# Holding stationary operands over consecutive matmuls, and loading four tiles ahead of the first store, in a running logsumexp

## The chip, the cores and the metric

One core of a Trainium2 chip. The metric is the time on the device in microseconds (us); medians of several runs are given, and of each kernel one execution was profiled. Ratios are the mean time of one kernel's fast runs over that of the other's of the same rounds, so they are not quite the ratio of the medians quoted beside them. The span of a profile is some 2 us shorter than the timed run.

## The reference, cut to what matters

```python
x: float32 [4, 4096, 4128]          # batch, sequence, columns
out[:, 0, :] = x[:, 0, :]
for t in range(1, 4096):
    mx = maximum(out[:, t-1, :], x[:, t, :])
    out[:, t, :] = mx + log(exp(out[:, t-1, :] - mx) + exp(x[:, t, :] - mx))
```

It is a running log of a running sum of exponentials along the sequence. 270.5 MB are read and as many are written.

## The kernel before

A tile ("step") is 128 partitions of three rows each (two in one step of each batch), 4128 columns wide: 6.34 MB in, and as many out, in the same buffer. ScalarE writes the exponentials as float16 over the tile, TensorE makes the running sums with triangular stationary operands (`incl`, `excl`, `ident`) and carries the last row over from the step before (`pick`), ScalarE takes the log back into the tile. There are four buffers.

```python
def mm(pt, w, rhs, start=False, stop=False):
    nc.tensor.matmul(pt, lhsT=w, rhs=rhs, start=start, stop=stop, skip_group_check=True)
...
for i in range(r):                       # small products of the last 32 columns
    e = self.e(i, CH, CH + tail)
    mm(qt[:, i:, :], incl, to(e, r - i), start=i == 0)
    if i:
        mm(qt[:, :i, :], excl, to(e, i))
...
ahead = bufs - 1                         # bufs = 4
for s in steps[:ahead]:
    s.load()
...
if k.c == last and d + 1 == k.t.r:       # the last piece of a step is done
    k.t.store()
    if stored + ahead < len(steps):
        steps[stored + ahead].load()
    stored += 1
```

All loads and stores are issued by SyncE, one after the other, into one queue that sixteen DMA engines serve.

The softmax here doesn't subtract the row's maximum and nothing guards it: scores larger than these inputs give would overflow.

## Time and profile before

| | before |
|---|---|
| time, median of the first 3 runs | 1262.91 us (1262.84 to 1263.04) |
| span of the profile | 1261.0 us |
| DMA queue, share of 16 engines | 99.4%, 541.07 MB |
| ScalarE / TensorE / weight loads / VectorE busy | 75 / 55 / 19 / 36% |

The views are read in the order: who is full (shares), what the compute engines wait for, in which order the queue is served, and what single stretches look like. The prediction shows those lines. The first is a row of the page's DMA queues (packets, MB, share), of a queue that carries no data of the kernel:

```profile
q8 instruction: 18, 0.29, 0.1%
```

A row of ScalarE's timeline: its first work on the last tile (start, duration, ..., and in brackets the idle time before and what ended it). It tells when the last load had landed:

```profile
1220.78 1.91 ACT L128 ACTIVATE xt<-xt 128x2048 f16<-128x2048 f32 x1 [1.34 <-DMA xt<-in_x_dram]
```

### The profile page before, as it was taken

What the parts mean: (1) busy time and instruction counts of PE and PEld (TensorE: products, weight loads), DVE (VectorE), ACT (ScalarE), POOL (GpSimd) and SP (SyncE); (2) the same over time, 40 slices, a digit from 0 to 9 for tenths busy, and PEclk for the clock granted to TensorE, in tenths of its full rate; (3) what the DMA queues carried; (4) which work ended last, traced back from release to release, by engine and by line L of the source; (5) the groups of instructions that cost most, each with busy time, mean ns of one, the idle gap of its engine ahead of it and who ended that gap; (6) DMA issues with size and microseconds to landing.
All of it is one profiled execution on the core that took longest, in us unless ns stands there. A gap on an engine that the chain in (4) does not pass through costs nothing.

```text
span 1261.0 us, 6165 instructions
## 1 busy us (share of the span) xinstructions
PE 688.7 (55%) x2268; PEld 237.0 (19%) x2268; DVE 451.4 (36%) x445; ACT 947.3 (75%) x733; POOL 2.2 (0%) x13
## 2 busy tenths in 40 slices
PE   3665554555555555655346555555634755664552
PEld 1222111111121111211112211111211211221120
DVE  2443333333333333334424333333442433333344
ACT  5997777777777777778569777777966977777794
POOL 0000000000000000000000000000000000000000
PEclk9887777777677777777768777787777777778786
DMA  9999999999999999999999999999999999999998
GB/s 411 410 439 431 432 427 434 438 430 432 433 437 431 432 432 436 432 427 436 431 433 436 437 429 431 436 436 432 430 434 435 432 431 432 434 435 431 433 422 347
DMA packets 12702, 541.46 MB, mean 429 GB/s; under 512 B 1408, under 2 KB 1408, under 8 KB 1408
## 3 DMA queue, kind: packets, MB, share of 16 engines
q1 hardware_dynamic: 12672, 541.07, 99.4%
q8 instruction: 18, 0.29, 0.1%
q14 instruction: 12, 0.10, 0.0%
HBM read 270.53 MB, written 270.53 MB: 429 GB/s over the span
## 4 chain that ended last, share of the span: by engine, by line
DMA 69%; ACT 21%; PE 5%; issue 2%; DVE 1%; SPq 0%; ACTq 0%
DMA xt<-in_x_dram 67%; ACT xt L128 11%; ACT xt L162 10%; PE pt L88 5%; DMA out_dram<-xt 2%; ACT xt L167 0%; SPq L116 0%; DVE carry L92 0%; DVE carry L93 0%; ACTq L231 0%; SPq L113 0%; ACTq L128 0%; PE qt L88 0%
## 5 line engine op out<-in xcount | busy, mean ns | idle before, releaser
L128 ACT ACTIVATE xt<-xt 128x3072 f16<-128x3072 f32 (+3 forms) x176 | 478.5, 2719 | 247.9 <-DMA xt<-in_x_dram 247.8
L88 PE MATMUL pt<-xt,ident 128*128 128x512 f16 x672 | 251.3, 470 | 530.7 <-ACT xt L162 530.4
L162 ACT ACTIVATE xt<-pt 128x1024 f32<-128x1024 f32 x512 | 487.6, 1030 | 2.5 <-PE pt L88 0.7
L92 DVE CAST carry<-pt 32x1024 f16<-32x1024 f32 x176 | 216.4, 1230 | 761.0 <-ACT xt L162 760.7
L88 PE MATMUL pt<-xt,excl 128*128 128x512 f16 x672 | 247.0, 504 | 0.0
L93 DVE TENSOR_TENSOR carry<-pt,carry 32x1024 f16<-32x1024 f32 x176 | 215.9, 1227 | 6.1
L88 PEld LDWEIGHTS <-ident 128*128 128x128 f16 x672 | 70.1, 104 | 677.7 <-issue 654.0
L88 PE MATMUL pt<-xt,incl 128*128 128x512 f16 x352 | 152.0, 526 | 23.6 <-ACT xt L128 15.0
L88 PEld LDWEIGHTS <-excl 128*128 128x128 f16 x756 | 92.5, 124 | 141.0 <-issue 108.1
L88 PE MATMUL pt<-carry,pick 128*128 128x512 f16 x320 | 109.8, 429 | 0.0
L88 PEld LDWEIGHTS <-incl 128*128 128x128 f16 x480 | 45.2, 111 | 129.7 <-DVE carry L93 95.2
L88 PEld LDWEIGHTS <-pick 128*128 128x128 f16 x360 | 40.6, 113 | 57.0 <-issue 34.3
L167 ACT ACTIVATE xt<-qt 128x96 f32<-128x96 f32 (+1 forms) x44 | 10.9, 249 | 45.7 <-PE pt L88 45.7
L92 DVE CAST carry_t<-qt 32x32 f16<-32x32 f32 x44 | 8.7, 197 | 25.5 <-ACT xt L167 25.4
L88 PE MATMUL qt<-xt,incl 128*128 128x64 f16 (+2 forms) x128 | 12.3, 196 | 0.0
L88 PE MATMUL qt<-xt,excl 128*128 128x64 f16 (+1 forms) x84 | 10.6, 187 | 0.0
L93 DVE TENSOR_TENSOR carry_t<-qt,carry_t 32x32 f16<-32x32 f32 x44 | 8.5, 193 | 1.5
L88 PE MATMUL qt<-carry_t,pick 128*128 128x96 f16 (+1 forms) x40 | 8.2, 204 | 0.0
L83 DVE MEMSET carry<- 128x512 uint32 x4 | 1.9, 485 | 1.1 <-PEq L220 1.0
L70 ACT ACT_TABLE_LOAD x1 | 1.3, 1283 | 0.8 <-PEq L220 0.8
L35 POOL TENSOR_SCALAR_AFFINE_SELECT pick<-pick 128x128 f16<-128x128 f16 x2 | 0.6, 294 | 0.1
L25 POOL TENSOR_SCALAR_AFFINE_SELECT incl<-incl 128x128 f16<-128x128 f16 x1 | 0.3, 294 | 0.0
(11 smaller groups left out, 1.9 us busy)
## 6 DMA issues: line engine op xcount, KB each, us to landing
xt<-in_x_dram SPq DMA_DIRECT2D x40, 6192.0 KB, 42.2
out_dram<-xt SPq DMA_DIRECT2D x40, 6192.0 KB, 28.1
xt<-in_x_dram SPq DMA_DIRECT2D x4, 4128.0 KB, 37.3
out_dram<-xt SPq DMA_DIRECT2D x4, 4128.0 KB, 23.0
```

Source lines behind the costliest of these rows:

```text
L25: nc.gpsimd.affine_select(out=t, in_=t, pattern=[[1, P]], compare_op=mybir.AluOpType.is_ge, fill=0.0, base=base, channel_multiplier=-1,)
L35: nc.gpsimd.affine_select(out=t, in_=t, pattern=[[step, P]], compare_op=mybir.AluOpType.not_equal, fill=1.0, base=base, channel_multiplier=1,)
L70: nc.scalar.preload_act_table_set("natural_log_exp_and_others")
L83: nc.vector.memset(t, 0.0)
L88: nc.tensor.matmul(pt, lhsT=w, rhs=rhs, start=start, stop=stop, skip_group_check=True)
L92: nc.vector.tensor_copy(cr[HI:HI + 32, :], pt[HI:HI + 32])
L93: nc.vector.tensor_tensor(out=cr[LO:LO + 32, :], in0=pt[HI:HI + 32], in1=cr[HI:HI + 32, :], op=mybir.AluOpType.subtract,)
L128: nc.scalar.activation(self.t.half[:, :, 2 * c0:2 * c0 + w], self.t.xt[:, :, c0:c0 + w], ACT.Exp,)
L162: nc.scalar.activation(t.xt[:, j, c * CH:(c + 1) * CH], pt, ACT.Ln)
L167: nc.scalar.activation(t.xt[:, :, t0:D], self.qt, ACT.Ln)
```

## The change

Its intent: a matmul that uses the same stationary operand as the one before it needs no weight load, and with four loads ahead of the first store each store is due one load later.

```diff
+    held = [None]
+
     def mm(pt, w, rhs, start=False, stop=False):
-        nc.tensor.matmul(pt, lhsT=w, rhs=rhs, start=start, stop=stop, skip_group_check=True)
+
+        if held[0] is not w:
+            nc.tensor.matmul(pt, lhsT=w, rhs=rhs, start=start, stop=stop, skip_group_check=True)
+            held[0] = w
+            return
+        pe = nc.tensor
+        pe.add_instruction(mybir.InstMatmult(
+            name=nc.get_next_instruction_name(),
+            ins=[pe.lower_ap(rhs), pe.lower_ap(w, for_matmul_weights=True)],
+            outs=[pe.lower_ap(pt, opt=True)],
+            start_tensor_calc=start, stop_tensor_calc=stop, ldweights=False,
+            tile_size=(P, P), tile_position=(0, 0), bass_skip_group_check=True,
+        ))
 ... (cut)
             for i in range(r):
-                e = self.e(i, CH, CH + tail)
-                mm(qt[:, i:, :], incl, to(e, r - i), start=i == 0)
-                if i:
-                    mm(qt[:, :i, :], excl, to(e, i))
+                mm(qt[:, i:, :], incl, to(self.e(i, CH, CH + tail), r - i), start=i == 0)
+            for i in range(1, r):
+                mm(qt[:, :i, :], excl, to(self.e(i, CH, CH + tail), i))
 ... (cut)
-    for s in steps[:ahead]:
+    for s in steps[:bufs]:
         s.load()
 ... (cut)
-                    if stored + ahead < len(steps):
+                    if bufs <= stored + ahead < len(steps):
                         steps[stored + ahead].load()
```

## The prediction

> **What bounds the kernel now.** I read the page's shares first, then its DMA rows, then the list of waits, then the DMA queue's own order of time, and last some stretches. In the shares no compute engine is full, while the sixteen DMA engines are, in all slices but the last; the one data queue holds 99.4% of the span:
>
> ```profile
> PE 688.7 (55%) x2268; PEld 237.0 (19%) x2268; DVE 451.4 (36%) x445; ACT 947.3 (75%) x733; POOL 2.2 (0%) x13
> ...
> DMA  9999999999999999999999999999999999999998
> ...
> q1 hardware_dynamic: 12672, 541.07, 99.4%
> ```
>
> The reader is to see two things: DMA is the bound, and there is one weight load for each matmul (2268 and 2268). The waits say on what the compute engines stand. ScalarE stood 247.8 us for loads, and 0.7 us for the main matmuls:
>
> ```profile
> ACT xt L128 <- DMA xt<-in_x_dram: 247.8, 42, 12.2
> ...
> ACT xt L167 <- PE pt L88: 45.7, 44, 1.1
> ...
> ACT xt L162 <- PE pt L88: 0.7, 1, 0.7
> ```
>
> So TensorE holds up ScalarE by 46.4 us at most, ScalarE waits five times as long for data, and the data comes at the rate of the queue. Third, the start of the DMA queue's order of time (start, duration of issuing, line):
>
> ```profile
> 0.80 1.33 SPq L113 DMA_DIRECT2D xt<-in_x_dram  x3
> 37.00 0.35 SPq L116 DMA_DIRECT2D out_dram<-xt  x1
> 37.39 0.44 SPq L113 DMA_DIRECT2D xt<-in_x_dram  x1
> 63.44 0.34 SPq L116 DMA_DIRECT2D out_dram<-xt  x1
> 63.88 0.38 SPq L113 DMA_DIRECT2D xt<-in_x_dram  x1
> 86.17 0.34 SPq L116 DMA_DIRECT2D out_dram<-xt  x1
> ```
>
> Call the loads L0, L1, ... and the stores S0, S1, ...; the order is L0 L1 L2, S0 L3, S1 L4, S2 L5, and so on. From there a pair comes every 29.25 us or so, and the page has 42.2 us from a load's issue to its landing and 28.1 us for a store. A load issued at time t lands at t + 42.2, and the next pair is issued at t + 29.25: at each new pair some 13 us of work still lie in the queue. It does not run dry. Fourth, three stretches (busy time of PE, PEld, DVE, ACT, POOL; granted clock, DMA share, GB/s): the end's gap, the last stores, and the long middle:
>
> ```profile
> 1226.00:1234.00 8.00, 5.18 (x17) 1.84 (x17) 3.32 (x6) 7.89 (x8) 0.00 (x0) 0.79 0.44 188
> 1234.00:1261.00 27.00, 4.99 (x24) 1.78 (x22) 12.31 (x12) 8.41 (x9) 0.00 (x0) 0.69 0.91 391
> 300.00:1200.00 900.00, 495.57 (x1626) 170.40 (x1626) 316.82 (x312) 675.84 (x522) 0.00 (x0) 0.76 1.00 433
> ```
>
> The middle runs at 433 GB/s with share 1.00. The whole time adds up from it. Bytes: 541.07 MB / 433 GB/s = 1249.6 us. Gap at the end, where the last but one store waits for its compute: 8 x (1 - 188/433) = 4.5 us. The last stores below the rate: 27 x (1 - 391/433) = 2.6 us. The first 100 us, at 419 GB/s by the same view: 100 x (1 - 419/433) = 3.2 us, start included. Sum 1259.9; the span is 1261.0, the timed median 1262.91 (1.9 us outside the span).
>
> **What the Trainium skill says.** "Perfetto Trace Analysis", Roofline, bounds a core that is alone by its 16 DMA engines, about 435 GB/s together; the trace agrees with 433 in the middle. "DMA: Bandwidth & Descriptors", Queues, rings and completion order, says that each DMA engine consumes the descriptors of a ring in order. The trace fits: three loads issued together at 0.80 come one after the other (ScalarE's first work on L0 starts at 13.08, on L1 at 27.68), so an order of issue is an order of service. "TensorE: Matmul & The Clock Gate", LDWEIGHTS, gives columns / 1.2 in ns, so 107 for 128 columns; the group of ident has 104. The same page, Architectural detail, says that PE pulls weight loads ahead of matmuls in flight. The trace shows them hidden: in
>
> ```profile
> 49.32 1.03 PE L88 MATMUL pt<-xt,excl 128*128 128x512 f16 x4
> 50.19 0.59 PE L88 MATMUL pt<-carry,pick 128*128 128x512 f16 x2
> ```
>
> four matmuls with a load each take (50.19 - 49.32) / 4 = 217 ns apiece at a clock of 1.00, which is 512 columns at 2.35 columns per ns and leaves no room for 104 ns of loading.
>
> **Part one, weights held.** By the diff a matmul with the same weights as the one before asks for no load. But the order in which the built program's instructions stand says otherwise. In the changed program, 816 matmuls are made by the old call and 1452 by the new branch, and all 2268 still have a weight load directly before them: 260 of incl, 536 of excl, 496 of ident and 160 of pick come from the new branch. Whatever builds the program puts a load before each matmul, flag or not. I therefore expect 2268 loads in the trace and 237 us of PEld as before. Were the loads gone, 260 x 111 + 536 x 124 + 496 x 104 + 160 x 113 ns (the means of the four groups) = 165 us of PEld would go, all of it beside matmuls. On the path: 0 us either way. What is real is that in the tail's small products all three incl ones now come before the three excl ones: 84 products of some 190 ns change places within groups of five or so, at the same count: 0 us.
>
> **Part two, L3 ahead of S0.** The listing of the queue has one row moved: L0 L1 L2 L3, S0, S1, L4, S2, L5. From S1 on the order is the same as before, with the same four buffers. So "each store one load later" holds for the first store alone; S1 comes after L0 to L3 in both. Step by step, from rows above: L1 landed at 27.68, a full tile takes 6.34 MB / 433 = 14.6 us and the small first one 9.8 us, so L2 lands at about 42.3. Before: S0 until 52, L3 until 66.7. After: L3 until 57, S0 until 66.7: the same bytes, swapped. S0 is still issued at 37.0 and S1 at 63.4, since ScalarE works without a pause from 27.68 to 93.6 in the trace, on data that has landed: it does not wait for L3. L4 needs S0 landed, as it takes its buffer; S0 lands some 3 us after S1 is issued, so L4 is issued at about 67 and no longer at 63.88. That is a new wait of 3 us, but S1's 14.6 us lie in the queue meanwhile: nothing runs dry, 0 us. S2 at 86.2 and L5 at 86.6 come as before, and the rest with them, the gap of 4.5 us at the end too.
>
> One small cost: the first 42 us hold loads alone. Their rows say 406 GB/s for 0 to 28 us and 396 for 28 to 42, so 16.9 MB in some 40 us after the start, 421 GB/s against 433. Loads alone for one more tile would cost 14.6 x (433/421 - 1) = 0.4 us. A second: at 63.4 only 3 us of S0 remain, and the DMA engines do not all end together (in the gap at the end their share falls over some 6 us, from 1226 to 1232); a few may idle a little. I put 0.1 us on that. In sum 0 + 0 + 0.4 + 0.1, less rounding and chance: 1263.2 us.
>
> **Rivals.** First, that the weight loads do go on the chip, and TensorE's path shortens. For it: the chain of waits has 5% of PE, 63 us. Against it: the chain goes back from L-loads whose issue waits for a store's compute, while the queue has 13 us in hand; the chain follows releases, not the bound. And the listing has all loads. It would make of the time 1262 to 1263, since at 100% DMA a faster TensorE only waits longer; at the end, where TensorE holds ScalarE by about 0.7 us a few times, perhaps 1 us less. Second, that the deeper start carries through and keeps the queue fuller, so that the gap at the end closes: 4.5 us less, 1258.4. Against it: the order from S1 on is the same, and the gap comes from the last tiles' compute after the last landing at 1220.8, not from the start. Third, that the new wait of L4 for S0 does dry the queue: S0 would have to land over 14 us after S1's issue. If it did, by as much as 5 us, 1268. Fourth, fewer loads alter the granted clock (0.76 in the middle): 0 us, as TensorE is not on the path.
>
> **Range and chances.** Runs of one kernel lie within 0.2 us here. The uncertainty is in how the DMA engines drift apart after the swap and how the gap at the end falls: about 2.5 us each way. So 1260.5 to 1266.0. For 2%, 25 us, DMA would have to lose or save 11 MB worth of time; no rival reaches it. Faster 0.01, within 0.98, slower 0.01.
>
> **What would show it right or wrong.** Right: 2268 weight loads and about 237 us of PEld; 433 GB/s in the middle; four loads issued at once at 0.8; S0 near 37, S1 near 63.4, L4 near 67, waiting for S0's store; S2 near 86; a gap of about 4.5 us near 1230. Step one is wrong if PEld shows 816 loads or some 72 us; step two if S1 or S2 moves by over 3 us, or if the DMA share falls below 0.9 anywhere before 1200. The prediction is wrong if the rate of the middle itself changes with the new order, which I have nothing against but the equal order of the queue.

## The result

The changed kernel takes 1262.76 us (1262.53 to 1262.87, 6 runs), the kernel before 1262.95 us (1262.84 to 1263.08, 6 runs). The ratio is 0.9998, with a 95% interval of 0.9985 to 1.0011: the same. The page of the changed kernel has the same shares, and as many weight loads:

```profile
PE 690.7 (55%) x2268; PEld 236.3 (19%) x2268; DVE 451.4 (36%) x445; ACT 947.0 (75%) x733; POOL 2.2 (0%) x13
...
q1 hardware_dynamic: 12672, 541.07, 99.4%
q8 instruction: 18, 0.29, 0.1%
```

PEld is 236.3 us in 2268 loads where it was 237.0 us in 2268: no operand is held on the chip. Its waits (engine and line, what it waited for, us in all, times, longest) answer to those of before one by one, under new line numbers:

```profile
ACT xt L142 <- DMA xt<-in_x_dram: 247.8, 42, 11.8
...
ACT xt L180 <- PE pt L96: 46.3, 44, 1.1
...
ACT xt L175 <- PE pt L96: 0.7, 1, 0.7
```

The start of its DMA queue, in order of time:

```profile
0.80 1.91 SPq L127 DMA_DIRECT2D xt<-in_x_dram  x4
37.23 26.77 SPq L130 DMA_DIRECT2D out_dram<-xt  x2
69.00 0.34 SPq L127 DMA_DIRECT2D xt<-in_x_dram  x1
86.40 0.33 SPq L130 DMA_DIRECT2D out_dram<-xt  x1
```

Four loads go out at once, S0 at 37.2 and S1 at 63.7 (the second of the row of two, which ends at 64.0 and takes 0.3 us). L4 goes out at 69.0 and no longer at 63.88. S2, at 86.4 for 86.17, is back in the old order. Last, the same three stretches as before, and the landing of the last tile:

```profile
300.00:1200.00 900.00, 493.75 (x1624) 168.74 (x1623) 316.83 (x311) 675.67 (x522) 0.00 (x0) 0.77 1.00 433
1226.00:1234.00 8.00, 5.96 (x17) 1.96 (x16) 2.92 (x5) 7.53 (x8) 0.00 (x0) 0.71 0.44 188
1234.00:1261.00 27.00, 5.40 (x24) 1.90 (x22) 12.67 (x12) 8.79 (x9) 0.00 (x0) 0.69 0.91 391
```

```profile
1220.72 1.91 ACT L142 ACTIVATE xt<-xt 128x2048 f16<-128x2048 f32 x1 [1.34 <-DMA xt<-in_x_dram]
```

The middle has 433 GB/s as before, the gap at the end 188 as before, and the last tile lands 0.06 us from where it landed.

### The profile page after: what moved, and what is told of

Same layout as the page of the kernel before. It is cut to its first block, busy times and chain, and to the rows that moved or that the text cites. A ratio compares the mean times of both kernels' runs of the same rounds, so it can differ in the third digit from the quotient of the medians.

```text
span 1261.0 us, 6165 instructions
## 1 busy us (share of the span) xinstructions
PE 690.7 (55%) x2268; PEld 236.3 (19%) x2268; DVE 451.4 (36%) x445; ACT 947.0 (75%) x733; POOL 2.2 (0%) x13
## 4 chain that ended last, share of the span: by engine, by line
DMA 72%; ACT 19%; PE 5%; issue 2%; DVE 1%; SPq 0%; ACTq 0%
DMA xt<-in_x_dram 67%; ACT xt L142 10%; ACT xt L175 9%; DMA out_dram<-xt 5%; PE pt L96 3%; PE pt L92 2%; DVE carry L106 0%; DVE carry L107 0%; ACT xt L180 0%; SPq L130 0%; ACTq L244 0%; SPq L127 0%; ACTq L142 0%; PE qt L92 0%
## 5 line engine op out<-in xcount | busy, mean ns | idle before, releaser
L142 ACT ACTIVATE xt<-xt 128x3072 f16<-128x3072 f32 (+3 forms) x176 | 478.2, 2717 | 247.9 <-DMA xt<-in_x_dram 247.8
L92 PE MATMUL pt<-xt,ident 128*128 128x512 f16 x176 | 76.6, 435 | 493.7 <-ACT xt L175 493.7
L96 PE MATMUL pt<-xt,ident 128*128 128x512 f16 x496 | 203.7, 477 | 35.4 <-ACT xt L175 34.7
L96 PE MATMUL pt<-xt,excl 128*128 128x512 f16 x496 | 187.6, 496 | 0.0
L92 PE MATMUL pt<-xt,incl 128*128 128x512 f16 x176 | 92.2, 524 | 23.5 <-ACT xt L142 15.1
L92 PE MATMUL pt<-xt,excl 128*128 128x512 f16 x176 | 93.4, 531 | 0.0
L96 PE MATMUL pt<-xt,incl 128*128 128x512 f16 x176 | 92.9, 528 | 0.0
L92 PE MATMUL pt<-carry,pick 128*128 128x512 f16 x160 | 72.0, 450 | 0.0
L96 PE MATMUL pt<-carry,pick 128*128 128x512 f16 x160 | 68.5, 428 | 0.0
L180 ACT ACTIVATE xt<-qt 128x96 f32<-128x96 f32 (+1 forms) x44 | 10.9, 248 | 46.3 <-PE pt L96 46.3
L92 PEld LDWEIGHTS <-incl 128*128 128x128 f16 x220 | 22.6, 103 | 118.0 <-DVE carry L107 95.3
L92 PEld LDWEIGHTS <-excl 128*128 128x128 f16 x220 | 26.8, 122 | 36.8 <-issue 27.9
L96 PEld LDWEIGHTS <-incl 128*128 128x128 f16 x260 | 27.8, 115 | 10.9 <-issue 4.8
```

Of the source, the lines that this page charges most:

```text
L96: pe.add_instruction(mybir.InstMatmult(name=nc.get_next_instruction_name(), ins=[pe.lower_ap(rhs), pe.lower_ap(w, for_matmul_weights=True) ...
L142: nc.scalar.activation(self.t.half[:, :, 2 * c0:2 * c0 + w], self.t.xt[:, :, c0:c0 + w], ACT.Exp,)
L180: nc.scalar.activation(t.xt[:, :, t0:D], self.qt, ACT.Ln)
```

## The experiments

The theory that I took in: the bytes at the rate of the DMA queue set the time, neither part of the change touches that, and the one place where compute holds up the queue is a gap of 4.5 us at the end. The rivals: TensorE's weight loads are on the path after all; two effects of the change cancel; the queue's lead matters. There were twelve runs, each with the kernel before on the same chip (1262.94 to 1262.98 us there).

### E1: the operands truly held

The load that the build puts before every matmul is taken out again where it repeats the one before, after the program is scheduled. The result is correct.

```diff
+    for f in nc.m.functions:
+        for b in f.blocks:
+            kept, last_w = [], None
+            for i in b.instructions:
+                if type(i).__name__ == "InstLdweights":
+                    w = str(i.ins[0])
+                    if w == last_w:
+                        continue
+                    last_w = w
+                kept.append(i)
+            if len(kept) < len(b.instructions):
+                b.instructions = kept
     r = _run(nc, [arrays], core_ids=[0])
```

> The changed kernel, with the 1452 repeated weight loads taken out of the built program, so that the intent of the change is met: 816 loads for 2268 matmuls. My theory (DMA sets the time, loads are hidden beside matmuls): PEld falls from about 236 us to 70 to 75 us, the time stays within 0.5 us of 1262.8, the middle stays at 433 GB/s, and ScalarE still waits about 248 us for loads of data. Rival (TensorE's part of the chain of waits is real time): 1262.8 less up to 20 us. A third outcome: at the end, where ScalarE waits for TensorE, up to 1 us is saved.

Measured: 1261.47 us (1261.41 to 1261.66, 5 runs), ratio 0.9988 (0.9976 to 1.0001). The times of the two kernels lie apart by 1.5 us with spreads of some 0.5 us, though the interval still touches 1. From its page, and its first work on the last tile:

```profile
PE 688.7 (55%) x2268; PEld 86.8 (7%) x816; DVE 451.4 (36%) x445; ACT 947.1 (75%) x733; POOL 2.2 (0%) x13
...
q8 instruction: 12, 0.20, 0.1%
```

```profile
1219.53 1.91 ACT L142 ACTIVATE xt<-xt 128x2048 f16<-128x2048 f32 x1 [1.17 <-DMA xt<-in_x_dram]
```

150 us of weight loads are gone, a little less than the 165 expected: that sum took the means of the four groups, and over all loads of before these come to 248.4 us where 237.0 were busy. The time falls by a hundredth of that, but by more than the 0.5 us that my theory allowed. It did not come through TensorE: ScalarE's waits for TensorE are as before (46.3 us for the small products, where before had 45.7). It came in the data: the last tile landed 1.25 us earlier. And the row of the instruction queue has 12 packets for 18.

### E2: every weight load twice

```diff
     def mm(pt, w, rhs, start=False, stop=False):
+        nc.tensor.ldweights(w)
         nc.tensor.matmul(pt, lhsT=w, rhs=rhs, ...)
```

> The kernel before, with one more weight load ahead of every matmul: 4536 loads. My theory: PEld doubles to about 470 us and the time stays within 1 us of 1262.9, as two loads of 104 ns still fit beside a matmul of 217 ns and as TensorE is not on the bound. Rival (weight loads are on the path): the time rises by a good part of 2268 x 104 ns = 236 us, at least 20 us.

Measured: 1267.30 us (1266.94 to 1267.92, 4 runs), ratio 1.0033 (1.0018 to 1.0049). Both expectations miss: 4.3 us is more than the 1 us of my theory and a small part of 236. PEld was busy for 341.5 us in 4536 loads, where 470 was expected. From its page and its timeline:

```profile
q8 instruction: 27, 0.44, 0.1%
```

```profile
1224.91 1.91 ACT L129 ACTIVATE xt<-xt 128x2048 f16<-128x2048 f32 x1 [1.44 <-DMA xt<-in_x_dram]
```

Again ScalarE's wait for the small products did not grow (45.5 us), and the last tile landed later, by 4.13 us. This pointed to another theory, F: TensorE's instructions are themselves fetched by the 16 DMA engines, in packets of 16 KB, and a kernel that fills these engines pays for them. "Runtime: NRT & Kernel Launch", Instruction fetch mechanics, has the refill in 16 KiB blocks of 256 instructions, by a DMA queue of the sequencer's own. The numbers agree: the trace of before has 4586 instructions of TensorE, so 17.9 blocks, and the page has 18 packets; E1's 3134 make 12.2, with 12 packets; E2's 6853 make 26.8, with 27.

### E3: the early load alone

The two lines of the diff on loads, on the kernel before; weights and order of matmuls untouched.

> The kernel before with only the fourth load put ahead of the first store; weights and order of matmuls untouched. My theory: the same as the changed kernel, 1262.8 within 0.4 us, with L4 issued near 69 us after a wait for S0 of some 5 us. Rival (two parts of the change of opposite sign cancel): the time differs from 1262.8 by 2 us or more.

Measured: 1262.84 us (1262.54 to 1263.10, 4 runs), ratio 0.9999 (0.9985 to 1.0013). As my theory had it: nothing cancels.

### E4: the last two tiles' stores cut by columns

```diff
+        def store_part(self, c):
+            a, z = c * CH, D if c == last else (c + 1) * CH
+            nc.sync.dma_start(out=self.dram(out)[:, :, a:z], in_=self.xt[:, :, a:z])
 ...
-                if k.c == last and d + 1 == k.t.r:
+                if k.t in steps[-2:]:
+                    if d + 1 == k.t.r:
+                        k.t.store_part(k.c)
+                elif k.c == last and d + 1 == k.t.r:
                     k.t.store()
```

> The kernel before, with the stores of the last two tiles cut into four by columns, each issued as soon as its columns are done. My theory (the gap of 4.5 us near 1230 is the only place where compute holds up the queue): the gap closes and the time falls by 3 to 4.5 us, to 1258.4 to 1260. Rival (the gap is the engines' uneven ends, or smaller pieces of 4 KB a row cost more than they save): 1262 or longer.

Measured: 1271.54 us (1270.99 to 1272.14, 5 runs), ratio 1.0069: slower by 8.6 us. The experiment failed in its making. ScalarE's timeline has a new wait, for a store of its own tile:

```profile
1253.50 1.96 ACT L132 ACTIVATE xt<-xt 128x2112 f16<-128x2112 f32 x1 [18.06 <-DMA out_dram<-xt]
```

The exponential of the last columns waited 18 us for the store of other columns. Three strided pieces of one tile interleave in address, and the pieces are taken to overlap by the program that places the waits (argued from the wait, not tested by itself). It says nothing about the gap; E11 repeats it with pieces that don't interleave.

### E5: a copy, without compute

```diff
-    stored = 0
-    chunks[0].exp()
-    ... (all of the pipeline)
+    for i, s in enumerate(steps):
+        s.store()
+        if i + ahead < len(steps):
+            steps[i + ahead].load()
```

> The kernel before with all compute left out: the same loads and stores in the same order through the same four buffers. The result is wrong on purpose (the output is a copy of the input). My theory (the bytes at the queue's rate set the time): only the gap at the end and a little drift go, so 1256 to 1260 us at 433 GB/s in the middle. Rival (compute in the pipeline holds the queue back all along): 1240 us or less.

Measured: 1258.83 us (1258.33 to 1259.63, 4 runs), ratio 0.9966 (0.9951 to 0.9981). Its output is wrong, which doesn't matter for the time. All compute together, with the fetch of its instructions, costs 4.1 us of 1263. So no change to TensorE has more than about that to gain while the bytes move like this. Its queues (packets, MB, share) have almost no fetch of instructions:

```profile
q1 hardware_dynamic: 12672, 541.07, 99.7%
q14 instruction: 1, 0.01, 0.0%
```

### E6: three buffers

```diff
-    bufs = 4
+    bufs = 3
```

> The kernel before with three buffers, so two loads ahead. My theory (a store is issued 15.9 us after the next tile's landing, and with four buffers some 13 us of queued work cover that): with three nothing covers it, the queue runs dry in every step, and a step takes 15.9 + 14.6 + 14.6 + about 2 = 47 us where it took 29.25, in all 1900 to 2050 us, with a DMA share of about 0.65 in the middle. Rival (the queue keeps itself full whatever the lead): within 5% of 1263 us.

Measured: 2018.63 us in one look. Its queue in order of time, two pairs, and a stretch in the middle:

```profile
318.96 0.34 SPq L116 DMA_DIRECT2D out_dram<-xt  x1
319.40 0.38 SPq L113 DMA_DIRECT2D xt<-in_x_dram  x1
366.48 0.34 SPq L116 DMA_DIRECT2D out_dram<-xt  x1
366.91 0.38 SPq L113 DMA_DIRECT2D xt<-in_x_dram  x1
```

```profile
900.00:1100.00 200.00, 62.47 (x205) 21.66 (x205) 41.85 (x42) 86.22 (x68) 0.00 (x0) 0.65 0.67 280
```

One pair comes 47.5 us after the other, where 47 were expected, and the DMA share over 900 to 1100 us is 0.67, where four buffers had pairs every 29.25 us and a share of 1.00. So the reading of the lead holds: with four buffers some 29 us of work (a store and a load) are queued when a tile lands, and 13 us are left when the next store is issued 16 us later; with three nothing is left. This is what a wait for the queue looks like when it counts; the changed kernel's wait of 5 us for S0 fell within the lead.

### E7 and E8: six smaller tiles, the real form of a deeper lead

E7 has `R = 2` and `bufs = 6` on the kernel before, E8 the stores cut by columns as in E4 on top.

> The kernel before with tiles of two rows a partition and six buffers, so five loads ahead of the first store: the real form of each store being due later. My theory: the middle stays at 433 GB/s, so a deeper queue gains nothing there; only the gap at the end, made by the last tiles' compute, shrinks by about a third: 1260 to 1263 us. Rival (a deeper lead keeps the DMA engines better fed): under 1258 us. Third: ScalarE, whose more numerous instructions bring it to some 1030 us busy, or VectorE become a hindrance: over 1266 us.

> Two rows a partition and six buffers, and the stores of the last two tiles cut into four by columns. My theory: what is left of the gap at the end closes, so it ends where the version with three rows and cut stores ends, within 1 us: 1258 to 1260 us. Rival (the smaller tiles cost at their borders): 1 us or more above that version.

Measured: E7 1264.30 us (1263.84 to 1264.36, 5 runs), ratio 1.0010 (0.9998 to 1.0023), so none of the three ranges: not faster with five loads ahead, and 1.4 us longer than the same number of bytes before. The middle had 433 GB/s. Here SyncE waits for the landing of stores in 58 loads, where the kernel before has 4 such waits:

```profile
SPq L113 <- DMA out_dram<-xt: 1083.9, 58, 19.7
```

That this costs the 1.4 us, since the slowest share of a store now times the queue, is argued and not tested.

E8 took 1282.93 us (1282.56 to 1284.00, 4 runs), with 41.6 us of ScalarE's waits for its own tile's stores in two waits: the fault of E4 again, and nothing else can be read from it.

### E9: idle instructions added

One instruction ahead of each matmul that counts up a semaphore that nobody waits for. This makes TensorE's stream as long as in E2, without a weight load more.

```diff
+    idle = nc.alloc_semaphore("idle")
 ...
     def mm(pt, w, rhs, start=False, stop=False):
+        nc.tensor.sem_inc(idle)
         nc.tensor.matmul(pt, lhsT=w, rhs=rhs, ...)
```

> The kernel before, with one more instruction ahead of every matmul that does nothing in the array: it counts a semaphore up that nobody waits for. TensorE's stream then is as long as in the run with loads twice (some 6800 instructions), but with 2268 weight loads. Theory F (the fetch of TensorE's instructions, 16 KB a packet on the same 16 DMA engines, 27 packets for 18, makes the slowest DMA engine later): the time rises as there, by 3 to 5 us, to 1266 to 1268, and ScalarE's waits for data grow by some 3 to 4 us. Theory T (the extra weight loads themselves held up TensorE): 1263 within 0.7 us.

Measured: 1266.32 us (1266.21 to 1266.51, 5 runs), ratio 1.0027 (1.0014 to 1.0039): theory F. From its page and its timeline:

```profile
PE 688.5 (54%) x2268; PEld 241.9 (19%) x2268; DVE 451.3 (36%) x445; ACT 947.8 (75%) x733; POOL 2.2 (0%) x13
...
q8 instruction: 26, 0.43, 0.1%
```

```profile
1224.05 1.91 ACT L130 ACTIVATE xt<-xt 128x2048 f16<-128x2048 f32 x1 [1.43 <-DMA xt<-in_x_dram]
```

There are 2268 loads as before, and still 3.4 us are lost; ScalarE's waits for data are 250.1 us for 247.8 (3 to 4 us more were expected), and the last tile lands 3.27 us later. Most of what E2 lost is thus the length of the stream.

### E10: held, with idle instructions in place of the loads

```diff
         pe = nc.tensor
+        pe.sem_inc(idle)
```

(on E1: 816 loads, 1452 idle instructions.)

> The changed kernel with the 1452 loads truly gone, and in the place of each the same idle instruction, so 816 loads but a stream as long as before (18 packets of fetch). Theory F: the 1.5 us that the real hold gained are lost again, 1262.5 to 1263.2. Theory T (the weight loads' time was what was gained): 1261.5 within 0.4 us.

Measured: 1264.89 us (1264.57 to 1265.62, 5 runs), ratio 1.0016 (1.0003 to 1.0028).

```profile
PE 681.5 (54%) x2268; PEld 85.6 (7%) x816; DVE 451.3 (36%) x445; ACT 948.0 (75%) x733; POOL 2.2 (0%) x13
...
q8 instruction: 18, 0.29, 0.1%
```

With 816 loads and 18 packets E1's gain is gone, as theory F says and theory T does not. But it overshoots F's range: 1.9 us more than before. Its last tile began at 1221.47, 0.7 us after that of before; the rest came after that. The trace's list of single packets shows most of this rest. The last fetch starts at 1246.8 us, among the last stores (before, it came at 1232.7, when most engines had run out of work). The engine that took it, followed packet by packet from there, is the one that ends last, at 1261.57; fourteen others end at 1259.60 to 1259.76. So it also counts when a packet comes.

### E11: the last two tiles' stores cut by rows

```diff
+        def store_row(self, j):
+            nc.sync.dma_start(out=self.dram(out)[:, j, :], in_=self.xt[:, j, :])
 ...
-                if k.c == last and d + 1 == k.t.r:
+                if k.t in steps[-2:]:
+                    if k.c == last:
+                        k.t.store_row(d)
+                elif k.c == last and d + 1 == k.t.r:
                     k.t.store()
```

> The kernel before, with the stores of the last two tiles cut by rows, each row issued once its last columns are done; unlike the cut by columns no row overlaps another in address, so no work on the tile waits for its own store. Theory S (the slowest DMA engine sets the end; in the gap near 1230 it is still busy, so that filling the gap for the other fifteen gains little): 1261.5 to 1263. Theory G (the gap is lost time of the queue): the time falls by 3 to 4.5 us, to 1258.4 to 1260.

Measured: 1263.45 us (1263.33 to 1263.67, 5 runs), ratio 1.0004 (0.9992 to 1.0017): the same as before, half a microsecond above the range of theory S and far from G. Two stretches of its end:

```profile
1226.00:1234.00 8.00, 5.66 (x17) 1.99 (x16) 2.99 (x5) 7.45 (x8) 0.00 (x0) 0.71 0.93 400
...
1255.00:1261.00 6.00, 0.00 (x0) 0.00 (x0) 0.00 (x0) 0.00 (x0) 0.00 (x0) 0.50 0.15 63
```

The gap is filled, 400 GB/s where it was 188, and nothing is gained: it comes back at the very end, at 63 GB/s. How many packets of the data queue are in flight, counted from the trace every 2 us, shows what it is:

```
us           1224 1226 1228 1230 1232 1234 1236 ... 1252 1254 1256 1258 1260
before         16   16   13    9    3    1   16 ...   16   16   16   16    0
rows (E11)     16   16   16   16   16   16   16 ...   16   16    4    3    1
copy (E5)      16   16   16   16   16   17   16 ...   11    7    2    0    0
```

In the kernel before the sixteen come to the end of S41 over some 8 us (1227.6 to 1235.1), and one packet is still in flight at 1234, when S42 has been issued (1233.63). The latest engine ends its share of S41 at 1235.12 and goes on with S42 at once: for it there is no gap. With the rows the same spread lies at the end of the run (twelve engines end by 1255.8, the last at 1260.03), and even the copy has it. The trace does not name the engine of a packet, but on a busy engine the next packet starts within some 3 ns of the end of the one before, so an engine can be followed; what E12 shows of the late ones is told there. Why the engines of the copy, without any fetch, drift apart is open.

### E12: the copy with idle instructions

E5 with 4536 `sem_inc` on TensorE's stream ahead of the loop.

> The copy without compute (wrong on purpose, the output is a copy of the input), with 4536 idle instructions on TensorE's stream, which brings back 18 packets of fetch, all early in the run. Theory F, with 0.25 to 0.5 us a packet as the two runs of the loads say: the copy's 1258.8 rises by 4 to 9 us; if the engine that fetches is not the one that ends last, less, 1 to 4. Theory T: 1258.8 within 0.7 us.

Measured: 1263.45 us (1263.35 to 1263.86, 5 runs), so 4.62 us above the copy, wrong like it.

```profile
q8 instruction: 17, 0.28, 0.1%
```

No matmul and no weight load runs here. Only idle instructions and their packets were added: 4.62 / 17 = 0.27 us a packet, and together more than the 4.1 us that all compute with its fetch cost in E5. The seven runs that bear most on theory F together:

| run | packets of fetch (q8) | median us | first work on the last tile |
|---|---|---|---|
| E5 copy | 0 | 1258.83 | |
| E12 copy, filled | 17 | 1263.45 | |
| E1 held | 12 | 1261.47 | 1219.53 |
| before | 18 | 1262.95 | 1220.78 |
| E10 held, filled | 18 | 1264.89 | 1221.47 |
| E9 filled | 26 | 1266.32 | 1224.05 |
| E2 loads twice | 27 | 1267.30 | 1224.91 |

By the last column a packet is worth (1220.78 - 1219.53) / 6 = 0.21 us from E1 to before, (1224.05 - 1220.78) / 8 = 0.41 us from before to E9, and 4.13 / 9 = 0.46 us to E2. Spread over sixteen engines at 433 GB/s a packet of 16,384 bytes would cost 0.04 us (worked out). The list of packets has what one costs its engine. The first of E12 (start and end in us, bytes), between two packets of data on the same engine:

```
data    32.896 -> 34.725   49536
fetch   34.722 -> 35.730   16384
data    35.716 -> 38.012   49536
```

A packet of data of this size takes 1.83 us as a rule; after the fetch it takes 2.30. So this engine is later by 38.012 - 34.725 - 1.83 = 1.46 us. In ten of the runs (the two kernels, E1 to E4 and E9 to E12), 162 of the 190 fetches stand between two packets of data in this way, and each cost its engine 1.27 to 1.56 us, with a median of 1.45. The other engines lose nothing: E12's first engines end at 1251.4, the copy's at 1251.8, but its last at 1260.4 for 1256.6. Followed back, this last one had three of the 17 fetches (at six places two engines fitted equally well). So a packet makes one engine late by some 1.45 us, and a tile has landed only when its last share has; how much of that reaches the time depends on which engine takes it and when. That lets one packet be worth 0.2 us in one run and 0.6 in another. The count of packets and that of instructions rise together in all of these runs, so it is this gap in the queue, not the counts alone, that speaks for the fetch.

## Why the prediction was right

**No operand is held.** The prediction read it off the built program, and the trace has 2268 loads and 236.3 us of PEld. The intent never reached the chip.

**The queue.** Four loads at once, S0 near 37, S1 near 63.4, S2 near 86 and the old order from there: all as worked out. L4 was put at about 67 after a wait of 3 us; it came at 69.0 after 5. The term was short by 2 us, since S0 counts as landed with its last share only: fifteen shares landed at 66.7 to 67.2, as predicted, and the sixteenth at 68.5, after a fetch packet on its engine at 59.8. S1's 14.6 us in the queue covered it. E3 shows this part alone to be worth nothing, E6 what an uncovered wait costs.

**The bound.** The sum of bytes and rate gave 1249.6 us; E5, with bytes alone, took 1258.83. The first two of the four rivals fell: E1 and E2 show that holding and doubling loads do not move ScalarE's waits for TensorE, E11 that a closed gap gains nothing. The third did not occur, and for the fourth the clock of the middle was 0.77 after 0.76.

**What was wrong inside a right sum.** Three terms. First, "loads alone" at 421 GB/s, which gave 0.4 us: the first 66 us moved 27.4 MB in both kernels (406 x 28 + 396 x 14 + 439 x 24 before, 406 x 28 + 453 x 14 + 405 x 24 after, in units of GB/s and us), so no such cost is there; rates over 14 us scatter (396 and 453 in the same stretch of the two kernels). Nor do the terms add up as written: 1262.9 + 0.4 + 0.1 is 1263.4, and the text puts 1263.2. Second, the gap of 4.5 us, counted as time that the queue lost: E11 filled it and the time stayed. It is the spread of the engines' ends; the latest engine had no gap. Third, the step "On the path: 0 us either way" for the weight loads. Held for real they were worth 1.5 us, and doubled they cost 4.3: not as work of TensorE, as the step rightly said, but as bytes of the program in the DMA engines, which the step left out. E9 and E12 show that. As the change removed no instruction, the omission did not touch the result.

**Is there a better version?** E1, the changed kernel with its intent met, is the only one under both: 1261.47 us, 0.12% less, with an interval that reaches 1.0001. The copy's 1258.83 is what is left to reach for while all bytes go through one core's queue in this way.

## What to carry to other kernels

Read in the built program, engine by engine, whether an intent such as "no load here" has survived, before working out what it is worth. In a kernel whose DMA engines are full, ask of each change only what it does to the bytes and to the order in the queue; the length of the instruction streams is part of the bytes, and here a packet of 256 instructions cost 0.2 to 0.6 us. A dip of the DMA rate near the end need not be time to win: count how many transfers are still in flight, since the last engine may have no gap at all.

## What the Trainium skill lacked or had wrong

- "Runtime: NRT & Kernel Launch", Instruction fetch mechanics, calls the cost of crossing a 16 KiB boundary "mostly hidden". It is right on the blocks (18 packets for 4586 instructions), and the waits of ScalarE for TensorE did not grow. It lacks that the fetch takes time from full DMA engines: some 1.45 us a packet on one engine, and 17 packets brought a plain copy from 1258.83 to 1263.45 us.
- "CRC Debugging", Comparing the Two Runs, has the refill of instructions on queue 14. Here the packets that follow the length of TensorE's stream are on queue 8 (12, 18 and 27 of 16 KB), and those on queue 14 did not change with it (12, and 13 in E9).
- No page has a figure for how far the 16 DMA engines drift apart on one long queue issued by SyncE: here they came to the end of one store over some 8 us, and to the end of the copy over 4.8 us (1251.8 to 1256.6).
- "TensorE: Matmul & The Clock Gate", Back-to-back issue gap, has some 131 ns a matmul in a stream of loads and matmuls of 512 columns; the trace of before has 217 ns at a clock of 1.00, which agrees with the isolated figure on the same page.
- No page says that the program's builder puts a weight load ahead of a matmul that asked for none: 2268 loads for 2268 matmuls, 1452 of which had asked for none.
